# A two-layer hybrid decoder: the first unit's attention held behind its value products on TensorE, with three padded stationaries

## The chip, the cores and the metric

The kernel runs on one core of one Trainium2 chip. The metric is the device time of one execution in microseconds. The kernel before has a median of 1480.25 us over three runs (1478.82 to 1484.95).

## The reference

Two layers work on 1040 tokens (16 meta tokens and 1024 real ones) of width 1024. Each layer normalises the tokens, projects them with one wide matrix to queries, keys, values, gates and forget logits, runs four heads of differential attention and eight heads of forgetting attention, gates the results, and adds an output projection to the tokens.

```python
u = rms_norm(h, norm_g)
proj = jnp.einsum('bld,dp->blp', u, w_in)
dq, dk, dv, dz, fq, fk, fv, fz, f_logit = jnp.split(proj, split_points, axis=-1)
...
p = probs(qa, k1) - lam * probs(qc, k2)          # four differential heads
o_a = einsum(p, v_a);  o_a = rms_norm(o_a, subln_g) * (1.0 - lambda_init)
...
s = q k * f_scale + c_q - cum;  o_b = softmax(s) v_f   # eight forgetting heads
mixed = jnp.concatenate([o_a * jax.nn.silu(dz), o_b * jax.nn.silu(fz)], axis=-1)
return h + jnp.einsum('blm,md->bld', mixed, w_out)
```

## The kernel before

A layer is cut into eight units of 128 projected columns: units 0 to 3 are one differential head each, units 4 to 7 two forgetting heads each. All eight k-tiles of the normalised tokens stay in SBUF as a high part `XTh` and a low part `XTl`. Every product of the projections is made three times (weight high by tokens high, weight low by tokens high, weight high by tokens low); line 357 issues them for queries, keys, gates and most values.

For unit 0 the order in the program is: keys (`project(ck, ...)`), queries (`project(cq, ...)`), values (`proj_v01`), then `attend`. `proj_v01` makes the values of units 0 and 1 and the forget logits together: first 16 products for the meta rows (line 416), then eight blocks of 128 tokens with 24 products each (line 437). Each block fills one bank of PSUM (`pj`), and ScalarE (line 441) and VectorE (lines 442 and 443) empty it. At its end the collected logits `fn` are transposed on TensorE (line 445). The four weight tiles of this step (`vwh`, `vwl`) come from the ring `e`, which has four places (`NE = 4`); the wide score tiles `E` of the attention come from the same ring.

The queries pass through ScalarE, DMAs that swap halves (`sw<-raw`), GpSimd (line 532), VectorE (lines 531 and 533) and are split into a high part `qa` and a low part `ql` (lines 546 and 539). Then a DMA on ScalarE's queue copies each half of `qa` beside itself (`qa<-qa`, line 149). A score matmul (line 710, or 830 for the meta rows) reads `qa` after that DMA; its second half (lines 712 and 831) reads a padded stationary: `low_queries` has GpSimd copy the two 64-row halves of `ql` into the two halves of a zeroed 128-row tile (line 693, two instructions). There are `NQZ` such tiles, in turn; they lie behind `XTl` in one tile of SBUF, and are zeroed once at the start (line 214). A score is then evicted by VectorE with the mask and a running minimum (line 716), made exponential by ScalarE (line 723), combined (line 734), transposed on TensorE (lines 875 to 901) and multiplied with the values (lines 797 to 820).

The order of instructions on each engine isn't the order of the program. A planner lays it out at build time: it models costs, gives each instruction a due time by the length of what hangs on it, and lets each engine take the most urgent instruction that its model holds to be ready. The engines then run these orders strictly. It also derives how many buffers a ring has where the program gives no count (the PSUM pools, `k`, `qa`, `ql`, `V`) from the room that is left. `tc.issue_after(ins)` binds the planner: what the block traces on the engine of `ins` is ordered behind `ins` on that engine; other engines aren't bound. `last_of(PE)` is the last TensorE instruction traced so far.

Of the kernel before, what the change touches and what calls it, by code (L numbers as in the profile page):

```python
# [16 lines left out]
PE = mybir.EngineType.PE  # L17
# [36 lines left out]
WLB = 6  # L54
VPB = 0
STB = 0
NQZ = 2
PMB = 4
OTB = 2
Q2B = 2  # L60
# [57 lines left out]
def hybrid_kernel(ctx: ExitStack, tc: tile.TileContext, x, meta, norm_g, w_in, b_forget,  # L118
# [18 lines left out]
    def last_of(engine):  # L137

        return next(i for i in reversed(nc.cur_bb.bb.instructions) if i.engine == engine)
# [4 lines left out]
    def dma(dst, src):  # L144
        nc.sync.dma_start(out=f32(dst), in_=f32(src))
# [50 lines left out]

    XT = [const.tile([P, KT * L + w], F32R, name=nm) for nm, w in (("XTh", 0), ("XTl", P + 2 * P * NQZ))]
    XTh, XTl = (x[:, 0:KT * L].rearrange("p (k t) -> p k t", k=KT) for x in XT)
# [15 lines left out]
    nc.gpsimd.memset(XT[1][:, qz0:].bitcast(F32), 0.0)  # L214
    qzs = [XT[1][:, qz0 + 2 * P * i:qz0 + 2 * P * (i + 1)].rearrange("p (m t) -> p m t", m=2) for i in range(NQZ)]
    nqz = [0]
# [131 lines left out]
    def run_late():  # L348
        while late:
            late.pop(0)()  # L350
# [315 lines left out]
    def unit_gate(l, U, from_dram):  # L666

        tq = U.tq
        cz = unit_cols(U.j)[3]
        if from_dram:  # L670
            OT = st("otl") if U.j in OTS and l == 0 else big.tile([P, L], F32, name="otl", tag="ot", bufs=OTB or None)
            dma(OT[:, tq:], ms[U.j][:, tq:])
        else:
            OT = U.OT

        def evz(ps, t0, n):
            gt = slot("ck")
            nc.scalar.activation(gt[:, :n], ps[:, :n], AF.Tanh, scale=0.5)
            nc.vector.scalar_tensor_tensor(out=gt[:, :n], in0=gt[:, :n], scalar=1.0,
                                           in1=ps[:, :n], op0=ALU.add, op1=ALU.mult)  # L680
            (nc.gpsimd if 'g' in ENG else nc.vector).tensor_tensor(out=OT[:, t0:t0 + n], in0=OT[:, t0:t0 + n], in1=gt[:, :n], op=ALU.mult)
        yield from proj(l, cz, CH_ALL if l == 0 else CH_REAL, evz)
        dma(ms[U.j][:, tq:], OT[:, tq:])

    def low_queries(U, t):

        if not U.diff:
            return [U.Qb[m][:, t:t + P] for m in range(2)]
        qz = qzs[nqz[0] % NQZ]
        nqz[0] += 1  # L690
# [236 lines left out]
    def sub_norm(U):  # L927

        tq = U.tq
        OT = U.OT  # L930
        cs = slice(0 if U.l == 0 else 1, 9)
        rsqrt(U.vr[:, 1, cs], U.vr[:, 0, cs], P, 9 - cs.start, U.vr[:, 2, cs])

        for t0, n, cols in ((0, NM, (0,)), (NM, 4 * P, (1, 2, 3, 4)), (NM + 4 * P, 4 * P, (5, 6, 7, 8))):
            if t0 < tq:
                continue
            ps = pt()
            w = min(n, P)
            for i, c in enumerate(cols):
                nc.tensor.transpose(ps[:, w * i:w * i + w], U.vr[0:w, 1, c:c + 1].to_broadcast([w, P]), ident[0:w, 0:w])  # L940
            o = OT[:, t0:t0 + n]
            nc.vector.scalar_tensor_tensor(out=o, in0=o, scalar=gsc[:, U.l, U.j:U.j + 1], in1=ps[:, :n],
                                           op0=ALU.mult, op1=ALU.mult)

    def drain(g):
        for _ in g:
            pass
# [72 lines left out]
    for l in range(DEPTH):  # L1020
# [5 lines left out]
        units = [Unit() for _ in range(8)]  # L1026
# [17 lines left out]
                setup_scalars()  # L1044
        for j in range(8):
            run_late()
            drain(attend(units[j]))
            here = Z_AT.get(j, [])
            if j < 7:
                if j >= 4 and j not in here:  # L1050
                    dma(ms[j][:, tq:], units[j].OT[:, tq:])
                drain(unit_proj(l, j + 1, units[j + 1], tabs))
            if j == 0:
                drain(forget(l))
            if j < 4:
                sub_norm(units[j])
                if j not in here:
                    dma(ms[j][:, tq:], units[j].OT[:, tq:])
            for jj in here:
                drain(unit_gate(l, units[jj], jj != j))  # L1060
# [162 lines left out]
```

## Time and profile before

| what | value |
|---|---|
| median of three runs | 1480.25 us |
| the profiled execution | 1482.97 us, of which its span is 1481.2 us |
| granted TensorE clock, mean over the span | 0.985 |
| instructions in the profile | 26901 |
| TensorE busy with matmuls | 1423.6 us (96%) |
| VectorE busy | 957.9 us (65%) |
| ScalarE busy | 700.0 us (47%) |
| GpSimd busy | 620.3 us (42%) |

The share of an engine is an average over stages with different limits. A row of a timeline gives start, duration, engine, line, operation, tiles and count, and in brackets how long the engine had been idle and what released it. Consecutive matmuls overlap in such rows, so the spacing of their starts is what a matmul costs.

### The profile page before, as it was taken

To read this page: it belongs to the slowest core of one execution; us is meant where nothing else is said; L and a number is where in the kernel's file an instruction comes from. 1 tells how busy PE (TensorE), PEld (TensorE's weight loads), DVE (VectorE), ACT (ScalarE), POOL (GpSimd) and SP (SyncE) were. 2 spreads that over 40 slices of the span, in tenths; PEclk is the share of its full clock that TensorE was granted. 3 is DMA by queue.
4 is the path that set the end of the run, shared out by engine and by line. 5 is a ranking of instruction groups with operands and counts; after the bars stand their busy time and mean duration, and the time that the engine had idled before them with its cause. 6 is when DMAs were issued, how large, how long until landed. Compare 5 with 4: busy or idle time off the path is not lost.

```text
span 1481.2 us, 26901 instructions
## 1 busy us (share of the span) xinstructions
PE 1423.6 (96%) x9282; PEld 1353.5 (91%) x9282; DVE 957.9 (65%) x2721; ACT 700.0 (47%) x1729; POOL 620.3 (42%) x1118
## 2 busy tenths in 40 slices
PE   7798999999999999999999989999999999999997
PEld 6798889999999999996888989899999999999886
DVE  7548787875666575654645678777657465655554
ACT  5236554545555465544222455544446455544521
POOL 4625544542445344663015335445324444445400
PEclk9899999999999999999999999999999999999999
DMA  8414331344322324447333232323431333253632
GB/s 199 92 27 57 56 59 43 62 44 73 77 65 52 78 35 88 99 145 178 119 127 70 30 56 51 58 58 60 56 89 30 74 63 68 56 110 99 207 133 90
DMA packets 112280, 119.64 MB, mean 81 GB/s; under 512 B 15440, under 2 KB 92880, under 8 KB 112144
## 3 DMA queue, kind: packets, MB, share of 16 engines
q1 hardware_dynamic: 106768, 105.14, 32.9%
q10 hardware_dynamic: 5376, 12.78, 3.5%
q8 instruction: 73, 1.20, 0.3%
q14 instruction: 63, 0.52, 0.1%
HBM read 70.92 MB, written 21.54 MB: 62 GB/s over the span
## 4 chain that ended last, share of the span: by engine, by line
PE 66%; DVE 5%; DMA 4%; ACT 2%; issue 2%; POOL 1%; SPq 1%; DVEq 0%; ACTq 0%; POOLq 0%
PE pj L357 31%; PE pss L1110 5%; PE pj L1110 5%; PE pt L885 3%; PE pss L710 3%; PE pss L712 3%; PE po L820 3%; PE po L819 2%; DMA wraw<-in_w_in_dram 1%; PE pj L437 1%; PE pt L1110 1%; DMA mt<-ms 1%; DMA sw<-raw 1%; DVE E L716 1%; PE po L817 1%
## 5 line engine op out<-in xcount | busy, mean ns | idle before, releaser
L357 PE MATMUL pj<-XTh,whi 128*128 128x346 f32 (+5 forms) x1392 | 453.8, 328 | 6.6 <-POOL whi L333 3.5
L357 PE MATMUL pj<-XTh,wlo 128*128 128x346 f32 (+5 forms) x1392 | 451.5, 325 | 0.9 <-POOL wlo L336 0.9
L357 PE MATMUL pj<-XTl,whi 128*128 128x346 f32 (+5 forms) x1392 | 450.7, 324 | 0.0
L357 PEld LDWEIGHTS pj<-XTh,whi 128*128 128x128 f32 x1392 | 263.7, 190 | 11.0 <-POOL whi L333 4.5
L357 PEld LDWEIGHTS pj<-XTh,wlo 128*128 128x128 f32 x1392 | 264.5, 190 | 2.2 <-POOL wlo L336 1.2
L357 PEld LDWEIGHTS pj<-XTl,whi 128*128 128x128 f32 x1392 | 263.9, 190 | 0.7
L716 DVE CUSTOM_DVE_ANT_0 E<-pss,cst 128x346 f32<-128x346 f32 (+6 forms) x384 | 212.1, 557 | 78.3 <-PE pss L712 64.9
L723 ACT ACTIVATE E<-E,cst 128x400 f32<-128x400 f32 (+2 forms) x192 | 172.4, 898 | 151.0 <-DVE cst L716 146.6
L336 POOL TENSOR_TENSOR wlo<-wraw,whi 128x256 fp32r<-128x256 f32 x232 | 180.8, 780 | 77.5 <-PE pj L357 64.1
L333 POOL TENSOR_SCALAR whi<-wraw 128x256 fp32r<-128x256 f32 x232 | 103.7, 447 | 220.1 <-DMA wraw<-in_w_in_dram 139.1
L794 DVE TENSOR_TENSOR ptl<-pt,pth 128x512 fp32r<-128x512 f32 (+1 forms) x240 | 147.3, 633 | 37.4 <-ACT pth L793 33.3
L710 PE MATMUL pss<-k,qa 128*128 128x400 f32 (+7 forms) x448 | 154.4, 350 | 12.4 <-DVE cst L716 7.7
L793 ACT CAST pth<-pt 128x512 fp32r<-128x512 f32 (+1 forms) x240 | 122.8, 545 | 73.0 <-PE pt L885 30.5
L740 POOL TENSOR_SCALAR E<-E,cst 128x400 f32<-128x400 f32 (+2 forms) x96 | 83.7, 873 | 102.6 <-DVE cst L739 99.1
L693 POOL TENSOR_SCALAR XTl<-ql 64x128 fp32r<-64x128 f32 x136 | 52.3, 387 | 130.7 <-PE pss L712 113.2
L710 PEld LDWEIGHTS pss<-k,qa 128*128 128x128 f32 x448 | 85.1, 190 | 19.4 <-DVE cst L716 12.3
L885 PE MATMUL pt<-cst,E 128*128 128x128 f32 x576 | 87.6, 275 | 0.3 <-DVE cst L716 0.2
L819 PE MATMUL po<-pth,V 128*128 128x256 f32 x320 | 82.5, 283 | 0.0
L820 PE MATMUL po<-ptl,V 128*128 128x256 f32 x320 | 81.6, 285 | 0.0
L712 PE MATMUL pss<-k,q 68*128 68x400 f32 (+6 forms) x224 | 71.8, 327 | 0.0
L712 PE MATMUL pss<-k,XTl 128*128 128x400 f32 (+6 forms) x224 | 71.7, 325 | 0.0
L885 PEld LDWEIGHTS pt<-cst,E 128*128 128x128 f32 x576 | 68.6, 143 | 2.5 <-DVE cst L716 0.8
(301 smaller groups left out, 2939.1 us busy)
## 6 DMA issues: line engine op xcount, KB each, us to landing
wraw<-in_w_in_dram SPq DMA_DIRECT2D x248, 128.0 KB
hb<-in_x_dram SPq DMA_DIRECT2D x16, 512.0 KB
wor<-in_w_out_dram SPq DMA_DIRECT2D x64, 128.0 KB
ms<-OT SPq DMA_DIRECT2D x8, 520.0 KB
k<-k ACTq DMA_DIRECT2D x16, 260.0 KB
h<-hb SPq DMA_DIRECT2D x8, 512.0 KB
ms<-OT SPq DMA_DIRECT2D x8, 512.0 KB
hb<-h SPq DMA_DIRECT2D x8, 512.0 KB
```

The costliest lines, as they stand in the source:

```text
L336: nc.gpsimd.tensor_tensor(out=lo, in0=raw, in1=hi.bitcast(F32), op=ALU.subtract)
L357: nc.tensor.matmul(ps[:, :n], lhsT=w, rhs=xx[:, k, t0:t0 + n], start=(k == 0 and i == 0), stop=(k == KT - 1 and i == 2))
L710: nc.tensor.matmul(ps[:, :nn], lhsT=U.Qa[m][:, t:t + P], rhs=U.K1[m][:, c0:c0 + nn], start=True, stop=False)
L712: nc.tensor.matmul(ps[:, :nn], lhsT=low[m], rhs=U.Kb[m][:, c0:c0 + nn], start=False, stop=True)
L716: nc.vector.tensor_tensor_reduce(out=E[:, c0:c0 + n], in0=ps[:, :n], in1=k, scale=-1.0, scalar=s[:, c - 1:c] if CHN and c else -NEG, op0=A ...
L723: nc.scalar.activation(E[:, :W], E[:, :W], AF.Exp, scale=-1.0, bias=lo, accum_out=s[:, 4:5])
L793: nc.scalar.copy(hi, ps)
L794: nc.vector.tensor_tensor(out=lo, in0=ps, in1=hi.bitcast(F32), op=ALU.subtract)
L819: nc.tensor.matmul(o[:, :256], lhsT=U.V[:, kb, hd, :], rhs=hi, start=False, stop=False)
L820: nc.tensor.matmul(o[:, :256], lhsT=U.V[:, kb, hd, :], rhs=lo, start=False, stop=last)
L885: nc.tensor.transpose(ps[:, (2 * a + b) * P:(2 * a + b + 1) * P], PP[:, k0:k0 + P], ident)
L1110: nc.tensor.matmul(ps, lhsT=xx[:, k, m0:m0 + P], rhs=wo[k][w][:, c], start=(k == 0 and i == 0), stop=(k == KT - 1 and i == 2))
```

## The change

The TensorE instructions of unit 0's attention are ordered behind the last TensorE instruction traced before it, in both layers. That instruction is the transpose of the forget logits (line 445), which follows the last value product. Instructions of other engines aren't bound. And the padded stationaries go from two to three, so `XTl`'s tile is 256 columns of 4 bytes wider in each partition, and one line of zeroing covers 768 columns where it covered 512.

```diff
-NQZ = 2
+NQZ = 3
...
         for j in range(8):
             run_late()
-            drain(attend(units[j]))
+            if j == 0:
+
+                with tc.issue_after(last_of(PE)):
+                    drain(attend(units[j]))
+            else:
+                drain(attend(units[j]))
             here = Z_AT.get(j, [])
```

## Rows read from the trace of the kernel before

**Rows 1.** The page's first part: busy time of each engine, share of span, instructions.
```profile
PE 1423.6 (96%) x9282; PEld 1353.5 (91%) x9282; DVE 957.9 (65%) x2721; ACT 700.0 (47%) x1729; POOL 620.3 (42%) x1118
```
**Rows 2.** Waits of TensorE over the span: line, releaser, us in total, times, longest.
```profile
PE pss L830 <- DMA qa<-qa: 6.8, 1, 6.8
PE pss L710 <- DMA qa<-qa: 3.8, 2, 3.3
PE pj L357 <- POOL whi L333: 3.5, 4, 1.8
```
**Rows 3.** Timeline of TensorE around the values of layer 0.
```profile
54.88 0.28 PE L437 MATMUL pj<-vwh,XTh 128*128 128x264 f32 x1
...
60.62 0.28 PE L437 MATMUL pj<-vwh,XTl 128*128 128x264 f32 x1
67.74 0.35 PE L830 MATMUL pss<-k,qa 128*128 128x16 f32 x1 [6.84 <-DMA qa<-qa]
...
68.90 0.35 PE L830 MATMUL pss<-k,qa 128*128 128x16 f32 x1 [0.60 <-DVE V L442]
...
70.13 0.42 PE L437 MATMUL pj<-vwh,XTh 128*128 128x264 f32 x1
...
87.98 0.28 PE L437 MATMUL pj<-vwh,XTl 128*128 128x264 f32 x1
...
89.57 0.32 PE L357 MATMUL pj<-XTh,whi 128*128 128x348 f32 x1
...
91.65 0.35 PE L710 MATMUL pss<-k,qa 128*128 128x400 f32 x1
91.83 0.34 PE L712 MATMUL pss<-k,XTl 128*128 128x400 f32 x1
...
93.76 0.27 PE L445 MATMUL pt<-cst 128*64 128x128 f32 x1
```
**Rows 4.** Busy time by stretch: length; PE, PEld, DVE, ACT, POOL; granted clock; DMA share, GB/s.
```profile
60.75:67.74 6.99, 0.15 (x2) 0.03 (x1) 6.80 (x12) 3.90 (x10) 4.13 (x7) 0.74 0.51 126
67.74:74.30 6.56, 5.96 (x25) 5.89 (x26) 1.98 (x10) 0.47 (x2) 2.77 (x7) 0.50 0.25 53
89.57:112.00 22.43, 22.43 (x147) 21.91 (x145) 14.60 (x52) 9.16 (x30) 10.47 (x19) 1.00 0.33 45
850.00:875.00 25.00, 19.01 (x114) 17.32 (x115) 22.29 (x52) 15.95 (x33) 11.66 (x19) 0.96 0.43 63
```
**Rows 5.** Timeline of TensorE around the values of layer 1.
```profile
800.88 0.28 PE L437 MATMUL pj<-vwh,XTl 128*128 128x264 f32 x1
804.51 0.43 PE L710 MATMUL pss<-k,qa 128*128 128x400 f32 x1 [3.35 <-DMA qa<-qa]
...
806.56 0.42 PE L437 MATMUL pj<-vwh,XTh 128*128 128x264 f32 x1
...
824.91 0.32 PE L357 MATMUL pj<-XTh,whi 128*128 128x348 f32 x1
```
**Rows 6.** Timelines of ScalarE and VectorE, layer 0: evictions of values, first score.
```profile
60.24 0.30 ACT L424 CAST Vm<-cst 16x128 fp32r<-16x128 f32 x1 [3.35 <-DVE cst L420]
...
59.74 0.41 DVE L420 TENSOR_TENSOR cst<-pj,cst 16x264 f32<-16x264 f32 x1
...
68.92 0.16 DVE L443 TENSOR_TENSOR cst<-pj,bfb 128x8 f32<-128x8 f32 x1
...
88.18 0.57 DVE L716 CUSTOM_DVE_ANT_0 E<-pss,cst 128x400 f32<-128x400 f32 x1
...
90.89 0.17 DVE L443 TENSOR_TENSOR cst<-pj,bfb 128x8 f32<-128x8 f32 x1
```
**Rows 7.** Timeline of VectorE, layer 1: first block's last eviction, first score.
```profile
805.93 0.16 DVE L443 TENSOR_TENSOR cst<-pj,bfb 128x8 f32<-128x8 f32 x1
...
823.52 0.57 DVE L716 CUSTOM_DVE_ANT_0 E<-pss,cst 128x400 f32<-128x400 f32 x1
```
**Rows 8.** Waits of GpSimd over the span, columns as in Rows 2.
```profile
POOL XTl L693 <- PE pss L712: 113.2, 38, 20.8
POOL whi L333 <- PE pss L712: 18.6, 7, 8.0
```

## The prediction, made before the changed kernel ran

> **What bounds the kernel now.** I read the page first. TensorE is busy for 96% of the span, and no other engine for more than 65% [rows 1]: the time is TensorE's work plus its idle time plus what it loses where its clock is low. The idle time is 1481.2 - 1423.6 = 57.6 us. So the next view is TensorE's waits over the span: among the longest are waits for the same small DMA, `qa<-qa`, one of 6.8 us at line 830 and one of 3.3 us at line 710 [rows 2]. Then the timelines around these two. In layer 0 the first two of the eight value blocks run from 54.88 to 60.74 us; then TensorE stands for 6.84 us before the meta scores of unit 0, whose high queries are not there yet, and for another 0.60 us before the second pair of them; the third value block starts only at 70.13 [rows 3]. In the stretch 60.75 to 67.74 TensorE has 0.15 us of work, and in the next 6.56 us the granted clock is 0.50, the lower of the two levels, 1.2 of 2.4 GHz [rows 4]. Layer 1 shows the same at 801.0 us: a gap of 3.35 us, scores, then the third block at 806.56 [rows 5]. Six value blocks that need none of these queries stand behind the waiting scores, because each engine runs its order strictly.
>
> What did the early scores bring? Little. VectorE takes the first wide score of layer 0 at 88.18, right after the twelfth product of the eighth block was issued at 87.98 [rows 3, 6]. The program explains it: a wide score tile comes from the ring `e`, whose four places hold the value weights, and the first of them comes free when the eighth block has used its first four k-tiles. In layer 1 the first score is taken at 823.52, 1.4 us before the first key product of unit 1 at 824.91 [rows 5, 7]. So the attention can't pass the values in either order; its early matmuls only waited in PSUM.
>
> **The change part by part.** (a) The edge on TensorE. It moves no work away, only back: in layer 0 four narrow meta matmuls and one pair of line 710/712; in layer 1 three pairs. One value product costs (60.62 - 54.88)/47 = 0.122 us at full clock, a pair 0.36 us (91.65, then 91.83, 0.18 apart) [rows 3]. With the narrow ones at the price of a value product, the moved work is 4 x 0.122 + 0.36 = 0.85 us in layer 0, and 3 x 0.36 = 1.08 us in layer 1.
>
> Layer 0: from the end of the second block (60.74) to unit 1's first key product (89.57) are 28.83 us, and the six blocks need 144 x 0.122 = 17.6. So 28.83 - 17.6 - 0.85 = 10.4 us of gap and low clock could go: that is the upper end. The lower end comes from PSUM. The third block very likely has a bank, since the meta rows' bank is emptied by line 420, which ends at 60.15 [rows 6]. The fourth may need the first block's bank, which VectorE releases only at 69.08 (line 443) [rows 6], since the evictions stand behind the splitting of the queries. Then it starts at 69.1, with five blocks of 2.93 us to go and again a low clock for as long as before, 6.56 us at half speed, a loss of 3.3: the end is 69.1 + 14.65 + 3.3 = 87.0, and the gain is 89.57 - 87.0 - 0.85 = 1.7 us.
>
> Layer 1: 824.91 - 801.0 = 23.9, less 17.6 and 1.08, gives at most 5.2. With the first block's bank free at 806.09 [rows 7], and the 0.8 us that low clock cost the products before (18.35 us from 806.56 to 824.91 for 17.6 us of work) [rows 5], the end is 806.1 + 14.65 + 0.8 = 821.5, and the gain 2.3 us.
>
> Between these ends I take two thirds of the way to the upper one. The reason is the planner: once the scores stand behind the values, the query splits are due later and the evictions sooner, and there is room for them: ScalarE stands for 3.35 us before 60.24, while the first block is complete at 57.8 [rows 6]. That makes 7.5 us in layer 0 and 4.2 in layer 1, 11.7 together (between 4.0 and 15.6).
>
> (b) What is late next: the start of the attention. Before, VectorE had the first score 1.5 us ahead of the end of the values (88.18 against 89.7). Now the first score is issued behind the transpose of the logits, and that waits for the eighth block's evictions, which ended at 91.06, 1.3 us behind the last product [rows 6]; with 0.2 us for the transpose and 0.36 for the pair the first score reaches VectorE about 1.9 us after the values. That is 3.4 us later against the end of the values, in each layer. Behind the waiting transpose on TensorE stand all scores of unit 0; who waits for them is VectorE's line 716, then ScalarE. The cover is unit 1's key products: in the 22.4 us behind the values TensorE is busy throughout [rows 4], so at first nothing is lost. Later the cover is gone: from 850 to 875 TensorE has 19.0 us of work in 25, with VectorE at 22.3 [rows 4], and there each us of delay counts. I take half: 1.7 us a layer, 3.4 in all, between 0 and the case in which the planner puts the transpose where it stands now, 4.0 us behind the last product at 93.76 [rows 3]: then 6.2 us a layer.
>
> The attention's first part issues no loads and stores of its own. The eight small DMAs of the logits stand behind the transpose on ScalarE's queue; they feed the forget gate, which only unit 4 reads, so I count nothing.
>
> (c) Three stationaries. GpSimd waits 113.2 us in all until a score has used the stationary that it is to overwrite, and after such a wait comes late to weight splits [rows 8]. TensorE in turn waits 3.5 us, in four waits, for such splits (line 333) [rows 2]; that is the most that could go. On the other side the planner may now put one more copy of two instructions, some 0.6 us, ahead of a split, 4 x 0.6 = 2.4 us if each of these waits grows so. I take a gain of 1 us. The 256 columns more to zero lie at the start, under the loading of the tokens: nothing. The kilobyte of SBUF costs no time by itself, but it is taken from the rings that the planner sizes (rival 3).
>
> **Sum.** 11.7 - 3.4 + 1 = 9.3 us off the span of 1481.2. The profiled execution took 1482.97, 2.7 us over the median of the three runs, and I carry the difference over to the median: 1480.25 - 9.3 = 1471.
>
> **Rivals.** 1. The banks hold the fourth block, and the wait for queries becomes a wait for evictions: 4.0 - 3.4 + 1 = 1.6 us, 1478.7. If even the third block has no bank, the gap stays as it is and the time is about 1481; this is the case in which the change doesn't do what it says. For it: the evictions do end late, at 69.08 and 806.09. Against it: the idle ScalarE above.
>
> 2. Slower: the attention's chain takes TensorE's place as the bound of each layer's first stage. The late start of up to 6.2 us is passed on in full in both layers, 12.4 us, while the values bring only the 4.0 us of the lower end: 8.4 us more, 1488.7. It decides from the point where the delay that TensorE can't fill is more than what the values give. For it: the stretch 850 to 875, where VectorE is fuller than TensorE. Against it: the 22.4 us without a gap in layer 0, and that the absolute start of the attention moves forward with the end of the values. A rule of the Trainium skill speaks for this rival (Perfetto Trace Analysis, section Identifying Performance Opportunities, Optimization Strategy): where the most-contended engine changes over the kernel, interleaving the two regimes helps; this change parts a VectorE-bound regime from a TensorE-bound one. By that rule the time would be this rival's. The trace agrees only in part: what was interleaved here were three pairs at most, and they bought no earlier eviction.
>
> 3. The plan moves elsewhere. New due times and a kilobyte less can give another order and other ring sizes anywhere. TensorE's idle time outside the two stretches is 57.6 - 10.8 = 46.8 us; if the plan shifts a fifth of it either way, that is 9 us on top of the forecast, 1462 to 1480.
>
> **How the numbers follow.** About 0.5% (7.4 us) is what a measurement of this kernel can tell from no change, so faster is under 1472.9 and slower over 1487.7. Forecast: 0.50, rival 1: 0.20, rival 2: 0.15, rival 3: 0.15. Faster: most of the forecast and a third of rival 3, 0.48. Slower: most of rival 2 and a little of 3, 0.16. The same: 0.36. The low end of the range takes the upper gain without any delay and a part of rival 3, 1480.25 - 15.6 - 3.5 = 1461; the high end reaches to rival 2, 1487.
>
> **What would show it.** Right: in both layers the value products run in one row at full clock with no wait for `qa<-qa`, the last ends near 79 to 83 us and near 819 to 821, the stretch behind 60 us has a clock of 1.00, and the waits for that DMA leave the list. Step (a) is wrong if a wait of line 437 for line 442 or 443 stands in its place. Step (b) is wrong if the first score at line 716 comes over 3 us behind the values, or TensorE's idle time grows in the 60 us behind them. Step (c) is wrong if waits for line 333 grow. The prediction as a whole is wrong if the gain is there at the end of the values and is lost before the output projection, or if later units' order differs and carries more than 5 us either way.

## The result, and the profile after

The changed kernel has a median of 1457.9 us over four runs (1455.0 to 1460.6), beside 1481.43 us (1478.82 to 1484.95) for the kernel before on the same chip: the ratio is 0.9835, with an interval of 0.982 to 0.985. It is 23.5 us faster. The forecast was 9.3 us, and 1457.9 lies 3 us under the low end of the range. The sign was right and the size was too small.

The profiled execution took 1455.0 us with a span of 1453.3. That is 28.0 us less than the profiled execution of before; of these, 4.4 us are the place of the two executions among their runs (before 1.5 us over its median, after 2.9 us under). The page's first part, busy time by engine:

```profile
PE 1412.7 (97%) x9282; PEld 1346.7 (93%) x9282; DVE 962.2 (66%) x2721; ACT 698.3 (48%) x1729; POOL 619.5 (43%) x1118
```

TensorE's idle time went from 57.6 to 1453.3 - 1412.7 = 40.6 us, and its busy time fell by 10.9 us for the same 9282 matmuls [rows 1]: less of it ran at the low clock (mean granted clock 0.993, before 0.985). Its longest waits over the span (line, releaser, us in total, times, longest), and those of GpSimd for a used stationary, beside [rows 2, 8]:

```profile
PE pt L294 <- DVE u L279: 5.9, 1, 5.9
PE po L797 <- DVE pm L809: 5.5, 4, 2.9
PE pj L357 <- POOL whi L333: 4.9, 4, 1.7
...
PE pss L710 <- DMA qa<-qa: 0.7, 1, 0.7
...
POOL XTl L693 <- PE pss L712: 74.0, 36, 17.0
...
POOL XTl L693 <- PE pss L831: 12.0, 2, 11.1
```

Of the 10.6 us of waits for the small DMA, 0.7 are left. Line 831 reads a stationary as line 712 does; the kernel before has 0.8 us of waits for it. So GpSimd's waits for a used stationary went from 114.0 to 86.0 us. TensorE's timeline in layer 0, where [rows 3] showed the gaps:

```profile
54.17 0.28 PE L437 MATMUL pj<-vwh,XTh 128*128 128x264 f32 x1
...
68.79 0.28 PE L437 MATMUL pj<-vwh,XTh 128*128 128x264 f32 x1
...
77.43 0.28 PE L437 MATMUL pj<-vwh,XTl 128*128 128x264 f32 x1
77.55 0.32 PE L357 MATMUL pj<-XTh,whi 128*128 128x348 f32 x1
...
81.39 0.27 PE L445 MATMUL pt<-cst 128*64 128x128 f32 x1
81.41 0.26 PE L830 MATMUL pss<-k,qa 128*128 128x16 f32 x1
...
81.86 0.43 PE L710 MATMUL pss<-k,qa 128*128 128x400 f32 x1
```

The eight blocks run in one row, 192 products from 54.17 to 77.55, with no gap. Then come 24 key products of unit 1, then the transpose, and the attention stands right behind it. Layer 1 is the same:

```profile
777.48 0.28 PE L437 MATMUL pj<-vwh,XTh 128*128 128x264 f32 x1
...
800.79 0.29 PE L437 MATMUL pj<-vwh,XTl 128*128 128x264 f32 x1
800.92 0.32 PE L357 MATMUL pj<-XTh,whi 128*128 128x348 f32 x1
```

Busy time by stretch (columns as in [rows 4]): the same two stretches of layer 0 as there, and in each layer the 60 us behind the values.

```profile
60.75:67.74 6.99, 6.99 (x60) 6.99 (x59) 5.79 (x11) 3.20 (x7) 3.61 (x8) 1.00 0.46 112
67.74:74.30 6.56, 6.56 (x56) 6.56 (x56) 4.19 (x22) 2.21 (x10) 2.53 (x4) 1.00 0.34 62
...
77.55:137.55 60.00, 56.61 (x362) 53.57 (x361) 47.28 (x138) 34.07 (x86) 29.19 (x54) 0.97 0.40 55
...
800.92:860.92 60.00, 56.76 (x371) 53.94 (x370) 48.02 (x130) 32.99 (x80) 29.12 (x54) 1.00 0.40 55
```

Where TensorE had 0.15 us of work in 6.99 and then a clock of 0.50, it is now full at a clock of 1.00. VectorE's evictions of the values (line 443) and its first scores (line 716), beside [rows 6, 7]:

```profile
69.04 0.16 DVE L443 TENSOR_TENSOR cst<-pj,bfb 128x8 f32<-128x8 f32 x1
...
78.88 0.17 DVE L443 TENSOR_TENSOR cst<-pj,bfb 128x8 f32<-128x8 f32 x1
...
82.50 0.57 DVE L716 CUSTOM_DVE_ANT_0 E<-pss,cst 128x400 f32<-128x400 f32 x1
...
805.41 0.57 DVE L716 CUSTOM_DVE_ANT_0 E<-pss,cst 128x400 f32<-128x400 f32 x1 [3.01 <-PE pss L712]
```

The first block's last eviction ends at 69.2, as before (69.08). At 68.79 the sixth block starts: five blocks lie in PSUM by then and not one is wholly emptied.

**Four lengths.** To see where the time went I divided each trace at four places on TensorE. "Values" runs from the first value product of a layer to unit 1's first key product behind them. "Out" runs from the 2041st product of line 357 to the 2161st: the end of layer 0's projections, its output projection and the way to layer 1's first product. "Whole" runs from the first to the last product of line 357, and "rest" is what is left of it. The start of the kernel and the last output projection are outside.

| kernel | counts | values 0 | values 1 | out | rest | whole |
|---|---|---|---|---|---|---|
| before | 2/3/4 | 34.7 | 29.7 | 133.1 | 1160.9 | 1358.4 |
| after | 2/3/4 | 23.4 | 23.4 | 133.3 | 1151.0 | 1331.1 |

The two values stages give 17.6 us. The moved scores cost 0.85 + 1.08 us by the prediction's prices and now stand in the rest; so the net gain there is 15.7 us. The rest gives 9.9 us although it holds 1.9 us more work. The column "counts" is what the planner settles on for three PSUM pools (`pj`/`pss`/`pt`): how many tiles of a pool may be alive at once in its model. They aren't the number of places on the chip, as the five blocks above show.

### The profile page after: what moved, and what is told of

Same layout as the page of the kernel before. It is cut to its first block, busy times and chain, and to the rows that moved or that the text cites. A ratio compares the mean times of both kernels' runs of the same rounds, so it can differ in the third digit from the quotient of the medians.

```text
span 1453.3 us, 26909 instructions
## 1 busy us (share of the span) xinstructions
PE 1412.7 (97%) x9282; PEld 1346.7 (93%) x9282; DVE 962.2 (66%) x2721; ACT 698.3 (48%) x1729; POOL 619.5 (43%) x1118
## 3 DMA queue, kind: packets, MB, share of 16 engines
q1 hardware_dynamic: 106768, 105.14, 33.9%
## 4 chain that ended last, share of the span: by engine, by line
PE 86%; DVE 6%; DMA 3%; ACT 2%; issue 2%; POOL 1%; SPq 1%; DVEq 0%; POOLq 0%; ACTq 0%
PE pj L357 42%; PE pss L1115 5%; PE pj L1115 5%; PE pss L710 4%; PE pss L712 4%; PE pt L885 4%; PE pj L437 3%; PE po L820 3%; PE po L819 3%; PE pt L1115 1%; PE po L817 1%; DMA wraw<-in_w_in_dram 1%; PE po L815 1%; DVE E L716 1%; PE po L816 1%
## 5 line engine op out<-in xcount | busy, mean ns | idle before, releaser
L723 ACT ACTIVATE E<-E,cst 128x400 f32<-128x400 f32 (+2 forms) x192 | 172.5, 898 | 133.4 <-DVE cst L716 129.4
L336 POOL TENSOR_TENSOR wlo<-wraw,whi 128x256 fp32r<-128x256 f32 x232 | 182.5, 787 | 42.3 <-PE pj L357 28.4
```

The lines of the kernel that those rows point to most:

```text
L336: nc.gpsimd.tensor_tensor(out=lo, in0=raw, in1=hi.bitcast(F32), op=ALU.subtract)
L723: nc.scalar.activation(E[:, :W], E[:, :W], AF.Exp, scale=-1.0, bias=lo, accum_out=s[:, 4:5])
```

## The experiments

Every diff is against the changed kernel. The same lengths for all of them, with the median and the ratio to the kernel before in the same batch:

| kernel | edge in layers, stationaries | counts | values 0 | values 1 | out | rest | whole | median, ratio |
|---|---|---|---|---|---|---|---|---|
| edge_l0 | 0, three | 2/3/4 | 23.4 | 29.5 | 133.3 | 1156.1 | 1342.3 | 1465.17, 0.988 |
| edge_l1 | 1, three | 2/3/3 | 34.0 | 23.4 | 150.1 | 1153.7 | 1361.4 | 1486.59, 1.004 |
| free3 | none, three | 2/3/3 | 33.9 | 30.2 | 151.3 | 1150.2 | 1365.6 | 1494.29, 1.009 |
| edge2 | both, two | 2/2/2 | 23.4 | 23.4 | 186.4 | 1202.9 | 1436.1 | 1569.89, 1.059 |
| before_pin | none, two | set to 2/3/4 | 33.6 | 29.7 | 130.4 | 1192.2 | 1385.9 | 1511.10, 1.020 |
| edge2_pin | both, two | set to 2/3/4 | 23.4 | 23.4 | 131.6 | 1199.1 | 1377.5 | 1501.56, 1.014 |
| free3_pin | none, three | set to 2/3/4 | 34.9 | 30.0 | 130.4 | 1188.2 | 1383.5 | 1505.68, 1.016 |
| after_pin | both, three | set to 2/3/4 | 23.4 | 23.4 | 128.2 | 1191.0 | 1366.0 | 1489.27, 1.004 |
| before_w40 | none, two | 2/3/4 | 35.4 | 31.7 | 133.4 | 1169.5 | 1370.0 | 1496.69, 1.009 |
| free3_w40 | none, three | 2/3/4 | 34.2 | 31.2 | 136.6 | 1159.6 | 1361.6 | 1490.71, 1.005 |
| after_w40 | both, three | 2/3/4 | 23.4 | 23.4 | 133.3 | 1159.5 | 1339.6 | 1469.90, 0.991 |
| mark7 | behind block 8, three | 2/3/4 | 24.2 | 24.4 | 133.1 | 1150.2 | 1331.9 | 1456.84, 0.983 |
| mark7_q2 | behind block 8, two | 4/4/4 | 24.6 | 24.7 | 162.4 | 1145.3 | 1357.0 | 1484.01, 1.001 |
| mark3 | behind block 4, three | 2/3/3 | 27.4 | 24.4 | 150.8 | 1147.9 | 1350.5 | 1479.37, 0.997 |
| edge4_w40 | both, four | 4/4/4 | 23.4 | 23.4 | 165.4 | 1152.7 | 1364.9 | 1496.57, 1.010 |

### The change in one layer alone, and in halves

The first question was whether each layer's edge gives what its values stage shows, and which half of the change carries the rest.

`edge_l0`:

```diff
-            if j == 0:
+            if j == 0 and l == 0:
```

> The edge in layer 0 alone, three stationaries. Gap theory (the gain is the stall and the low clock in the values of each layer): layer 0's values run in one row, 11 to 12 us less, and layer 1 keeps its gap of 3.3 us at line 710: 1469 to 1470 us. Plan theory (a good part of the gain comes from another order everywhere, set off by the change): the time differs from that by over 4 us either way. Stationary theory (the third stationary itself brings some 5 us, by fewer waits of GpSimd at line 693): 1464.

Measured: 1465.17 us (1462.74 to 1467.14), ratio 0.9882 [0.9855, 0.991]. Layer 0's values take 23.4 us and layer 1 still has its gap, in TensorE's timeline:

```profile
791.70 0.67 PE L710 MATMUL pss<-k,qa 128*128 128x400 f32 x1 [3.35 <-DMA qa<-qa]
```

The edge's effect on the values is local: the gap stays exactly where the edge is not. The time is 4 to 5 us under the 1469 to 1470 of the gap theory and 1 us over the stationary theory's 1464, so something outside the values is gained too.

`edge_l1`:

```diff
-            if j == 0:
+            if j == 0 and l == 1:
```

> The edge in layer 1 alone, three stationaries. Gap theory: layer 0 keeps its stall of 6.8 us, layer 1 loses its 3.3 us and the low clock behind it, 5 to 6 us less: 1475 to 1476. Plan theory: in this build the planner gives the PSUM ring pt three places where the kernels before and after have four, so the rest of the kernel has another order, and the time is off the 1475 by over 4 us, more likely upward. Stationary theory: 1470.

Measured: 1486.59 us (1484.72 to 1488.40), ratio 1.0037 [1.0022, 1.0052]. The values of layer 1 gain the same 6.3 us as in the full change, and yet the kernel isn't faster: "out" is 17.0 us longer, long before layer 1's values begin. The planner settled on other counts, 2/3/3, as the plan theory expected.

`free3`:

```diff
-            if j == 0:
-                with tc.issue_after(last_of(PE)):
-                    drain(attend(units[j]))
-            else:
-                drain(attend(units[j]))
+            drain(attend(units[j]))
```

> Three stationaries and no edge. Gap theory: both gaps stay, 1481, no change. Stationary theory: GpSimd's waits at line 693 fall from 113 us towards 75, and some 5 us are gained, 1476. Plan theory: pt has three places here as well, and the order differs everywhere: off by over 4 us either way from 1481 with both gaps still in the trace.

Measured: 1494.29 us (1492.30 to 1497.71), ratio 1.0087 [1.0062, 1.0112]. The third stationary alone comes out slower, with the same counts of 2/3/3 and the loss in the same place: 18.2 us more in "out", against 10.7 us less in the rest.

`edge2`:

```diff
-NQZ = 3
+NQZ = 2
```

> The edge in both layers with two stationaries. Gap theory: the whole gain of the values, 1463 to 1465. Stationary theory: the same less its 5 us, that is 1463, with GpSimd's waits at line 693 as before. Plan theory: in this build the planner stops early with two places for pss and two for pt instead of three and four, so scores and transposes wait for banks through both layers: slower than before, over 1500.

Measured: 1569.89 us (1565.31 to 1571.43), ratio 1.0589 [1.0563, 1.0616]. The edge alone makes the kernel 88.8 us slower, although both values stages take the same 23.4 us as in the full change: they give 17.6 us and the plan takes 53.3 us in "out" and 42 us in the rest. Here the planner settled on only two tiles of `pss` and two of `pt`. The halves can't be added: the edge alone costs 88.8 us and the third stationary alone 13.2, and the two together bring 23.5. What these runs compare is plans.

### The same counts for all four

`before_pin`, `edge2_pin`, `free3_pin` and `after_pin` set the four pools to the counts which the kernels before and after both have:

```diff
-PSB = (0, 0, 0, 0)
+PSB = (2, 3, 4, 1)
```

with the edge taken out as in `free3` for `free3_pin`, `NQZ = 2` for `edge2_pin`, and both for `before_pin`.

> The kernel before with the PSUM rings given as the planner itself had sized them for it (pj 2, pss 3, pt 4, po 1). Base of a comparison of four kernels in which the rings can't move. Plan theory: near 1481 us, within 6, with both gaps in the values. Gap theory: 1481.

> The edge in both layers, two stationaries, the same fixed PSUM rings; unpinned the planner had given pss two places and pt two and the kernel took 1570 us. Ring theory (those 89 us are the two small rings and nothing else): the rings are back, so about 17 us under before_pin, 1463 or so. If two stationaries hurt by themselves when the attention is held back: still over 1480. Stationary theory: 5 us over after_pin.

> Three stationaries without the edge, the same fixed PSUM rings; unpinned pt had three places and the kernel took 1494 us. Ring theory: with pt at four the loss around layer 0's output projection (17 us) is gone, and the time is that of before_pin within 4 us. Stationary theory: 5 us under before_pin. If the third stationary hurts by itself: still 10 us over.

> The changed kernel (edge in both layers, three stationaries) with the same fixed PSUM rings. Gap theory: 17.6 us less in the two value stages, so about 17 under before_pin. Plan theory in its strong form (what the change gained beyond the value stages, some 6 us, is the order of the rest): the gain against before_pin is anywhere from 10 to 25. Stationary theory: 22 to 24, as between the free kernels.

Measured: 1511.10, 1501.56, 1505.68 and 1489.27 us; ratios 1.0203 [1.018, 1.0225], 1.0138 [1.0116, 1.0159], 1.0161 [1.0142, 1.018] and 1.0044 [1.0023, 1.0064]. Two things follow. To write down the counts that the planner had found by itself costs 30 us: with fixed counts it lays another order, and the rest is 31 us longer. No theory had expected that. And among the four the change keeps its worth: the edge gives 9.5 us with two stationaries and 16.4 with three, the third stationary 5.4 us without the edge and 12.3 with it, both together 21.8. The edge's 9.5 us are well short of the 17 which the ring theory gave `edge2_pin`; the 5.4 and the 21.8 are close to what the stationary theory gave. But its reason doesn't hold: GpSimd's waits for a used stationary (lines 712 and 831 together) are 110.6 us in `before_pin` and 112.1 in `free3_pin`, and 95.5 in `edge2_pin` and 90.7 in `after_pin`. It is mainly the edge that shortens them, not the third tile.

### The same counts, found by the planner

`before_w40`, `free3_w40` and `after_w40` make the warm-up products at the start longer, with which the planner settles on 2/3/4 for all three:

```diff
-WARM = 30
+WARM = 40
```

> The kernel before with 40 instead of 30 matmuls in the warm-up on TensorE at the start. The ten more cost nothing by themselves (TensorE stands for 1.76 us after the warm-up, and ten take 1.5), but they give the planner other numbers; the PSUM rings come out as in the kernel before. Base for two others with the same warm-up and the same rings. Gap and stationary theory: 1481. Plan theory: within 10 us of 1481, and the difference to 1481 is what the plan alone is worth.

> Three stationaries, no edge, the longer warm-up: here the rings are those of the kernel before without being given. Stationary theory: 4 to 6 us under before_w40 (as with the given rings: 1505.7 against 1511.1). Plan theory: within 10 us of before_w40 on either side; a loss would say that the 5 us were chance.

> Edge in both layers and three stationaries, the longer warm-up, the same rings. Gap theory: 17 us under free3_w40 (16.4 with the given rings). Stationary theory: 22 us under before_w40. Plan theory: 17 with an error of 10.

Measured: 1496.69, 1490.71 and 1469.90 us; ratios 1.0092 [1.0066, 1.0118], 1.0047 [1.0028, 1.0065] and 0.9912 [0.9886, 0.9937]. With the longer warm-up the kernel before is 14 to 15 us slower, where the ten products more were expected to cost nothing; 10.8 of them lie ahead of the first value product (65.70 instead of 54.88 us). TensorE's longest wait for the normalised tokens (line 279) is 10.6 us there, and 5.4 in the kernel before. Behind that the plans are close to those of before and after, and the halves can be told apart: the third stationary gives 6.0 us (in the profiled pair 9.9 us less of rest and 3.2 more in "out"); the edge on top gives 20.8, 18.6 of them in the two values stages; together 26.8.

### When the attention starts

`mark7` holds the attention behind the last value product instead of the transpose, `mark3` behind the fourth block of eight:

```diff
+    vmark = {}
...
+            if b == 7:
+                vmark[l] = last_of(PE)
...
-                with tc.issue_after(last_of(PE)):
+                with tc.issue_after(vmark[l]):
```

(in `mark3` the condition is `b == 3`; in both, line 437 is line 438, and from line 441 on the numbers are three higher).

> The changed kernel with the attention held behind the last value product itself in place of the transpose of the logits that follows it: the scores no longer wait for the last block's evictions, and the first comes some 2 us earlier against the end of the values. The rings come out as in the changed kernel. If the late start of the attention costs (step b of the prediction, half of 3.4 us a layer): up to 3.4 us under the changed kernel's 1457.9. If unit 1's key products cover it: the same, within the plan's error.

Measured: 1456.84 us (1455.53 to 1460.82), ratio 0.9832 [0.9802, 0.9863], against 0.9835 [0.982, 0.985] for the changed kernel. VectorE's first scores:

```profile
78.54 0.57 DVE L719 CUSTOM_DVE_ANT_0 E<-pss,cst 128x400 f32<-128x400 f32 x1 [0.22 <-PE pss L715]
...
806.62 0.56 DVE L719 CUSTOM_DVE_ANT_0 E<-pss,cst 128x400 f32<-128x400 f32 x1
```

They come 0.2 us behind and 0.3 us ahead of unit 1's first key product; in the changed kernel it is 4.95 and 4.49 us behind. In `mark7` that key product itself stands behind the first scores; against the last value product the scores came 3.9 us sooner in layer 0 and 3.8 in layer 1. The time is the same. In layer 0 the order behind them was 2.4 to 3.2 us ahead of the changed kernel from the 361st to the 601st product of line 357, had lost it by the 721st and was 7.2 us behind at the 841st; in layer 1, whose values it reached 5.0 us behind the changed kernel, it was 8.2, 9.0 and 4.6 us behind at the 2401st, 2521st and 2641st. So a price of a late start of up to 3 us in layer 0 isn't excluded, but it isn't found in the total.

> The attention held only behind the fourth value block, where the copied queries should just have landed; the planner then puts the meta scores and a first pair between the fourth and the fifth block, as it had put them between the second and the third before. pt has three places here, so the whole time is expected near free3's family, 1470 to 1485, and the verdict is in the value stage. Gap theory: the stall goes as in the changed kernel, to within 1 us, and the values end at 78 to 79 us. Interleaving rule: the first score at line 716 comes clearly earlier against the end of the values, and TensorE's idle time behind them is lower. Ring e theory: the first wide score still waits for the eighth block, 1.5 us ahead of the end of the values, and nothing is won.

Measured: 1479.37 us (1475.98 to 1483.47), ratio 0.9973 [0.9956, 0.999], with counts of 2/3/3 and 17.7 us more in "out" than the kernel before. What the run was for is the values stage of layer 0. TensorE's timeline, then its stretches, then VectorE's first score and its third in layer 1, and last that third score in the kernel before:

```profile
67.62 0.28 PE L438 MATMUL pj<-vwh,XTl 128*128 128x264 f32 x1
68.39 0.25 PE L833 MATMUL pss<-k,qa 128*128 128x16 f32 x1 [0.49 <-DMA qa<-qa]
...
69.29 0.25 PE L833 MATMUL pss<-k,qa 128*128 128x16 f32 x1 [0.54 <-DMA qa<-qa]
...
70.19 0.29 PE L438 MATMUL pj<-vwh,XTh 128*128 128x264 f32 x1
...
83.41 0.32 PE L357 MATMUL pj<-XTh,whi 128*128 128x348 f32 x1
...
68.00:70.00 2.00, 0.97 (x5) 0.88 (x6) 1.94 (x7) 0.64 (x3) 1.83 (x4) 1.00 1.05 189
70.00:74.00 4.00, 4.00 (x23) 4.00 (x23) 1.62 (x11) 0.70 (x3) 2.04 (x6) 0.63 0.02 4
...
82.02 0.57 DVE L719 CUSTOM_DVE_ANT_0 E<-pss,cst 128x400 f32<-128x400 f32 x1
...
824.82 0.43 DVE L719 CUSTOM_DVE_ANT_0 E<-pss,cst 128x264 f32<-128x264 f32 x1 [0.39 <-PE pj L438]
...
824.98 0.43 DVE L716 CUSTOM_DVE_ANT_0 E<-pss,cst 128x264 f32<-128x264 f32 x1 [0.39 <-PE pj L437]
```

The values end at 83.4 us and not at the 78 to 79 of the gap theory; 1.9 us of that are their later beginning (56.04 instead of 54.17). The first score is ready at 70.4 us and VectorE takes it at 82.02, 1.4 us ahead of the end of the values: just the distance of the kernel before (88.18 against 89.57). The same 1.4 us stand in layer 1, and in every kernel here whose scores are issued between the blocks. By itself this distance doesn't name the ring `e`, for in VectorE's order the first score also stands right behind the seventh block's evictions. The third score of layer 1 does: it needs a third tile of the ring, its score matmuls were issued by 812.89, VectorE stands idle ahead of it, and it waits 0.39 us for one of the last value products. In the kernel before it is the same. So the ring `e` holds the attention back until the values' last block, as the prediction had it, and scores between the blocks buy 1.6 us at most against `mark7`, counted from unit 1's first key product (2.4 from the last value product). They cost more: two waits of 0.49 and 0.54 us, and behind them a granted clock of 0.63 in the next 4 us, so that the last four blocks take 13.2 us where `mark7` and the changed kernel need 11.7.

### Two stationaries and four

`mark7_q2` is `mark7` with

```diff
-NQZ = 3
+NQZ = 2
```

and `edge4_w40` is `after_w40` with `NQZ = 4`.

> The kernel mark7 with two stationaries in place of three; the attention is held back just as far. Here the planner does not stop early: pj, pss and pt have four places each, where mark7 has two, three and four. Stationary theory (with the attention held back the third stationary is worth 10 us or so, as with the given rings, 1489.3 against 1501.6): 1466 to 1469. Ring theory (edge2's 89 us were the small rings alone, and the stationaries bring next to nothing by themselves): 1457 within 5.

> Edge in both layers, four stationaries, the longer warm-up; pj, pss and pt have four places. Against after_w40 (three stationaries, 1469.9). If GpSimd's lead over the scores is what a stationary brings: some us less, 1465 to 1469, with GpSimd's waits at line 693 lower again. If three suffice: 1470 within the plan's error of 10.

Measured: 1484.01 us (1481.41 to 1487.57), ratio 1.0013 [0.9996, 1.003]; and 1496.57 us (1494.77 to 1501.28), ratio 1.0103 [1.0066, 1.0139]. Both were to say how the time goes with the number of stationaries, and neither does: in both the planner settled on 4/4/4, and "out" is 29 and 32 us longer than in their partners. TensorE in two stretches of 50 us ahead of and in the output projection, first `mark7`, then `mark7_q2`:

```profile
650.00:700.00 50.00, 48.65 (x216) 36.45 (x215) 26.73 (x57) 21.22 (x55) 19.81 (x24) 1.00 0.68 168
700.00:750.00 50.00, 50.00 (x242) 41.04 (x241) 31.97 (x90) 14.23 (x36) 0.00 (x0) 1.00 0.37 129
```

```profile
650.00:700.00 50.00, 46.68 (x245) 38.03 (x244) 32.20 (x74) 30.37 (x74) 24.88 (x39) 0.93 0.49 131
700.00:750.00 50.00, 47.06 (x214) 36.87 (x213) 26.10 (x75) 11.93 (x32) 6.18 (x10) 0.97 0.40 115
```

The second has 4.9 us less of TensorE work in these 100 us, and a mean clock below full in both halves. Two of its waits in this part (columns as in [rows 2]) are for the last unit's score and for an output weight:

```profile
PE pss L713 <- DVE cst L719: 3.3, 1, 3.3
PE pj L1113 <- POOL wo_ot L1086: 2.9, 1, 2.9
```

`edge4_w40` has the same two waits, of 3.3 and 4.2 us. In the rest `mark7_q2`, with two stationaries, is the quickest of all: 1145.3 us, 5 us under `mark7`. But `edge4_w40`, with four and the same counts of 4/4/4, has a rest 6.8 us under its partner's too, so this may be the counts. Neither run shows what a stationary is worth, and the 12.3 us which the third gave under the edge in one plan are not shown to be its own.

## Why the prediction was right or wrong

**The bound and the cause** stand. The time was TensorE's work, its idle time and its low clock. Holding back some matmuls that waited for a small DMA closed both gaps, and in the eight kernels that have the edge the values take 23.4 us in every layer that has it, whatever the plan.

**Step (a), values.** Counted at 11.7 us, between 4.0 and 15.6. It is 15.7 net, the upper end. What failed is the lower end: I let the fourth block wait for the first block's bank, which comes free at 69.1. It came free at 69.2 and no block waited, for five of them lay unemptied in PSUM. The trace of before had no row on how many banks the values have. Nor did the planner empty the blocks sooner, which was my reason for two thirds of the way; no cover was needed. So the weighing between the ends was the mistake, and 4.0 us of it.

**Step (b), the late start.** By its own criterion it was wrong: I expected the first score some 1.9 us behind the values and it came 4.95 and 4.49 us behind unit 1's first key product (4.8 and 4.3 behind the end of the last value product), since the planner put 24 key products of unit 1 ahead of the transpose. That is about the far end I named, for which I had 6.2 us a layer. The price did not follow: in the 60 us behind the values TensorE has 56.61 and 56.76 us of work where the kernel before had 55.44 and 53.90:

```profile
89.57:149.57 60.00, 55.44 (x354) 52.70 (x352) 46.27 (x135) 32.71 (x82) 30.12 (x51) 0.97 0.39 54
824.91:884.91 60.00, 53.90 (x346) 51.67 (x345) 47.99 (x131) 33.52 (x80) 25.52 (x48) 0.97 0.29 46
```

At the 361st product of line 357 the changed kernel is 12.0 us ahead of the kernel before, as at the end of layer 0's values; at the 2641st it is 24.4, and at the end of layer 1's values it was 24.0. And `mark7`, with 3.9 us less of the delay, takes the same time. The delay is one against the end of the values only: counted from the first value product, the first score comes after 28.3 and 27.9 us in the two layers, where it was 33.3 and 28.4. The term of 3.4 us was too much by about that; with plans that differ by several us in between, a rest of it can't be excluded. That the ring `e` gates an early start held in `mark3` too.

**Step (c), the third stationary.** Counted at 1 us, between -2.4 and +3.5. Its mechanism isn't there: TensorE's waits for weight splits went from 3.5 to 4.9 us, and GpSimd's shorter waits come mainly from the edge. And yet a third stationary without the edge is worth 5.4 us in one plan and 6.0 in another with equal counts. I can't name the wait that it removes; the gain is spread over the units, and the rest is also 10.7 us shorter in `free3` and 15.6 us shorter in `mark7_q2`, which has two stationaries. The range of this step was too narrow because it held only what the step itself does.

**Sum.** With medians 23.5 us, of which 15.7 are (a) and 7.8 everything else, where I had -2.4. So of the 14.2 us between forecast and measurement 4.0 are the size of (a), 11.7 taken and 15.7 measured, and 10.2 lie outside the values: the 3.4 us of (b), a price that no run shows, and 6.8 us beyond the 1 us of (c), for which the sum had no term: it took a move of the plan at nothing. The low end of the range held 3.5 us of such a move. How the 7.8 us divide between the third stationary and the plan stays open. In the profiled pair the idle time outside the values fell from 46.8 to 40.6 us; of the 10.9 us of busy time, 4.9 lie in the values (53.6 us there before, now 46.8 and the 1.9 of the moved scores), so some 6 us more went elsewhere, which fits the higher mean clock but isn't traced stretch by stretch.

**Rival 1** (banks) fell: no wait of line 437 appears. **Rival 2** (the attention's chain as the bound) fell too: the first score came 6.3 and 5.9 us later against the values than before, and had that been passed on in full, 5.4 of the 17.6 us would be left. At most some 3 us of it, in layer 0, aren't excluded (`mark7`). The rule of the Trainium skill that spoke for it (Perfetto Trace Analysis, section Identifying Performance Opportunities, Optimization Strategy: performance may be improved by interleaving the regimes) gets no support from these runs: `mark3` interleaves, and its attention starts no more than 2.4 us sooner than in `mark7`, because the values hold the ring that the scores need; in layer 0 it pays 3.2 us for that (27.4 against 24.2). **Rival 3** (the plan moves elsewhere) is what happened on top of the forecast, to the good side, by about the 9 us that I gave it. Its chance stood at 0.15; the experiments showed moves of 17 to 53 us in the one stretch "out", and of 30 and 88 us in the total, from edits of a few numbers. It should have set the width of the range.

**What stays open.** Why counts of 4/4/4 and of 2/3/3 cost 17 to 32 us at layer 0's output projection; the longest waits there are 3 to 4 us and explain only a part. What a third stationary is worth under the edge in a plan with equal counts: only one plan has the pair. And which part of the 9.9 us of rest belongs to the third stationary and which to chance in the plan.

## What to carry to other kernels

In a queue that runs strictly in order, look for a waiting instruction that stands ahead of ready work, and ask what the early instruction buys: where its consumer lacks a buffer until later anyway, hold it back; here the gain was the upper end of what the rows allowed, because no row showed what would be late next and nothing was. Where a planner lays out the order at build time, an edit's local effect could here be forecast within 4 us and the plan's move could not: read the planner's counts first, compare kernels with equal counts and in more than one plan, and give the move of the plan a width from measured edits. A helper edit that looks like nothing (here a third tile) may be what keeps the planner in a good plan, so the halves of such a change should not be judged one by one.

## What I had not expected of the hardware

Two stops of half a microsecond were followed by the low clock. In `mark3` TensorE stood for 0.49 and 0.54 us, with narrow matmuls around, had 0.97 us of work between 68 and 70 us, and was then granted 0.63 in the mean over the next 4 us; that cost 1.5 us on four blocks, more than the two stops together. In the kernel before, 6.84 us of standing still were followed by 6.56 us at 0.50 [rows 4]. And PSUM held five unemptied value blocks at once, where I had thought of three.
